# Masked softmax of x·W: another start order, strided transposes, and 16 KB runs over four batches

## The chip, the cores and the metric

The kernel runs on one core of a Trainium2 chip. The metric is the device time of one execution in microseconds (us). Instructions run on five engines: PE (matrix multiply, with its weight loads shown apart as PEld), DVE (VectorE), ACT (ScalarE), POOL (GpSimd) and SP (SyncE, which only issues transfers here). Transfers run on sixteen DMA engines.

## The reference

```python
batch, m, k, n = 16, 512, 512, 512          # x: (16,512,512) f32, weight: (512,512) f32
"scale": np.float32(0.125)
"mask": (np.triu(np.ones((m, n))) == 0).astype(np.float32)   # 1 strictly below the diagonal

y = scale * np.matmul(x, weight)
y = np.where(mask == 1, y, -1e9)
y_max = np.max(y, axis=-1, keepdims=True)
y_exp = np.exp(y - y_max)
return (y_exp / np.sum(y_exp, axis=-1, keepdims=True)).astype(np.float32)
```

Row 0 of every batch is masked everywhere, so its softmax is 1/512 in every column. In rows 0 to 255 the columns from 256 on are masked and their result is zero.

## The kernel before

**Units.** The work is cut into 16 units of 512 rows. A unit takes one half `h` (256 rows) of two neighbouring batches. Partition `2p+e` of the unit's tile holds four consecutive rows (`T = 4`) of batch `e`, so that one partition reads and writes one run of 4 x 2 KB = 8 KB in DRAM. Even units are the upper half (`h = 0`), for which only the first 256 columns of the product are computed ("narrow"); odd units are the lower half, with all 512 ("wide").

**Steps of a unit.** `load` (L78) brings 1 MB of x as float32. `cast` (L83, DVE) makes it bfloat16. `transpose` (L92, PE) makes 16 transposes of 128x128: each loads a slice of `xb` as the stationary operand and streams the identity through. `evict` copies them from PSUM to `xt`, half on DVE (L102), half on ACT (L103). `multiply` makes, for each of the four row slots, four matmuls with W (L116), one with the identity as stationary operand that adds -512 where the mask is 0 (L125, from `band`), and the exponential on ACT with the row sum (L135); no maximum is subtracted. `normalise` (DVE, L150 and L152) multiplies by the reciprocal of the sum and, in narrow units, POOL writes 1/512 into row 0 (L154). `store` (L158) writes 1 MB, with zeros in the columns that narrow units don't compute, which were put there once.

**Order.** The order on each engine is the program's order (`seq`). The main loop makes, for each `u`: transpose(u+1), cast(u+2), evict(u+1), multiply(u), normalise(u-1), store(u-1), load(u+7). All transfers are issued by SP, so they stand in one order: x's unit 0, W, the mask's diagonal blocks, x's units 1 to 7, and then stores and loads by turns.

**Start.** POOL builds the identity, the matrix `spread` (eight selections, L173), fills `band` with its constants (L182, L183) and four output tiles with zeros (L185, L186). W is loaded with row `kt*128+p` in partition `p`, that is four runs of 2 KB a partition, and cast in four pieces, two on DVE (L193), two on ACT (L195). The four 128x128 blocks on the mask's diagonal come in one DMA; `diag_bf` (L197) turns 0/1 into -512/0, and four matmuls with `spread` (L209) bring its rows to the partitions where the row slots of a unit stand; DVE and ACT copy them to `band` (L216).

**Buffers.** Eight x tiles and eight output tiles of 1 MB, three each of `xb` and `xt`, four PSUM banks for the transposes and four for the products.

Of the kernel before, what the change touches and what calls it, by code (L numbers as in the profile page):

```python
# [8 lines left out]
FP32 = mybir.dt.float32  # L9
BF16 = mybir.dt.bfloat16  # L10
AF = mybir.ActivationFunctionType
ALU = mybir.AluOpType

MASK_NEG = -512.0
P = 128
X_BUFS = 8
OUT_BUFS = 8


@with_exitstack  # L20
def kernel(
    ctx: ExitStack,
    tc: tile.TileContext,
    x: bass.AP,
    weight: bass.AP,
    scale: float,
    mask: bass.AP,
    out: bass.AP,
):

    nc = tc.nc  # L40

    B, M, K = x.shape
    K2, N = weight.shape
    assert K == K2 and N == 512 and K == 512 and M == 512 and B % 2 == 0
    KT = K // P
    T = 4
    HP = P // 2
    HB = 2 * P
    U = B

    const = ctx.enter_context(tc.tile_pool(name="const", bufs=1))
    x_pool = ctx.enter_context(tc.tile_pool(name="xf", bufs=X_BUFS))
    xb_pool = ctx.enter_context(tc.tile_pool(name="xb", bufs=3))
    xt_pool = ctx.enter_context(tc.tile_pool(name="xt", bufs=3))
    sum_pool = ctx.enter_context(tc.tile_pool(name="sums", bufs=4))
    psum_t = ctx.enter_context(tc.tile_pool(name="psum_t", bufs=4, space=bass.MemoryType.PSUM))
    psum_y = ctx.enter_context(tc.tile_pool(name="psum_y", bufs=4, space=bass.MemoryType.PSUM))

    x_r = x.rearrange("(c e) (h p t) k -> c h p e (t k)", e=2, h=2, t=T)
    out_r = out.rearrange("(c e) (h p t) n -> c h p e (t n)", e=2, h=2, t=T)  # L60

    diag_r = bass.AP(tensor=mask.tensor, offset=mask.offset, ap=[[N, P], [P * N + P, KT], [1, P]])

    ident_bf = const.tile([P, P], BF16, name="ident_bf")
    w_f32 = const.tile([P, KT, N], FP32, name="w_f32")
    w_bf = const.tile([P, KT, N], BF16, name="w_bf")
    diag_f32 = const.tile([P, KT, P], FP32, name="diag_f32")
    diag_bf = const.tile([P, KT, P], BF16, name="diag_bf")
    spread = const.tile([P, T, P], BF16, name="spread")
    band = const.tile([P, 2, T, HB], BF16, name="band")  # L70
    ots = [const.tile([P, T, N], FP32, name=f"ot{i}") for i in range(OUT_BUFS)]

    st_x, st_xb, st_pt, st_xt, st_sum = {}, {}, {}, {}, {}
    seq = tc.keep_in_program_order

    def load(u):
        xf = x_pool.tile([P, T, K], FP32, name="xf")
        seq(nc.sync.dma_start(xf.rearrange("p t k -> p (t k)"), x_r[u // 2, u % 2]))  # L78
        st_x[u] = xf

    def cast(u):
        xb = xb_pool.tile([P, T, K], BF16, name="xb")
        seq(nc.vector.tensor_copy(xb, st_x.pop(u)))  # L83
        st_xb[u] = xb

    def transpose(u):
        xb = st_xb.pop(u)
        st_pt[u] = [psum_t.tile([P, 2, T, P], BF16, name="pt") for _ in range(2)]
        for kt in range(KT):
            for t in range(T):  # L90
                seq(
                    nc.tensor.transpose(  # L92
                        st_pt[u][kt // 2][:, kt % 2, t],
                        xb[:, t, kt * P : (kt + 1) * P],
                        ident_bf,
                    )
                )

    def evict(u):
        xt = xt_pool.tile([P, KT, T, P], BF16, name="xt")  # L100
        pt = st_pt.pop(u)
        seq(nc.vector.tensor_copy(xt[:, 0:2], pt[0]))  # L102
        seq(nc.scalar.copy(xt[:, 2:4], pt[1]))  # L103
        st_xt[u] = xt

    def multiply(u):
        h = u % 2
        NC = (h + 1) * HB
        xt = st_xt.pop(u)
        ot = ots[u % OUT_BUFS]  # L110
        rsum = sum_pool.tile([P, T], FP32, name="rsum")
        for t in range(T):
            py = psum_y.tile([P, N], FP32, name="py")
            for kt in range(KT):
                seq(
                    nc.tensor.matmul(  # L116
                        py[:, :NC],
                        lhsT=xt[:, kt, t],
                        rhs=w_bf[:, kt, :NC],
                        start=(kt == 0),  # L120
                        stop=(kt == KT - 1),
                    )
                )
            seq(
                nc.tensor.matmul(  # L125
                    py[:, h * HB : NC],
                    lhsT=ident_bf,
                    rhs=band[:, h, t],
                    start=False,
                    stop=True,  # L130
                    skip_group_check=True,
                )
            )
            seq(
                nc.scalar.activation(  # L135
                    out=ot[:, t, :NC],
                    in_=py[:, :NC],
                    func=AF.Exp,
                    bias=0.0,
                    scale=float(scale),  # L140
                    accum_out=rsum[:, t : t + 1],
                )
            )
        st_sum[u] = rsum

    def normalise(u):
        ot = ots[u % OUT_BUFS]
        NC = (u % 2 + 1) * HB
        rinv = sum_pool.tile([P, T], FP32, name="rinv")
        seq(nc.vector.reciprocal(rinv, st_sum.pop(u)))  # L150
        for t in range(T):
            seq(nc.vector.tensor_scalar_mul(ot[:, t, :NC], ot[:, t, :NC], rinv[:, t : t + 1]))  # L152
        if u % 2 == 0:
            seq(nc.gpsimd.memset(ot[0:2, 0, :HB], 1.0 / N))  # L154

    def store(u):
        ot = ots[u % OUT_BUFS]
        seq(nc.sync.dma_start(out_r[u // 2, u % 2], ot.rearrange("p t n -> p (t n)")))  # L158


    load(0)
    seq(nc.sync.dma_start(w_f32, weight.rearrange("(kt p) n -> p kt n", p=P)))
    seq(nc.sync.dma_start(diag_f32, diag_r))
    for u in range(1, X_BUFS):
        load(u)

    make_identity(nc, ident_bf)


    nc.gpsimd.memset(spread, 0.0)  # L170
    for t in range(T):
        for g in range(2):
            nc.gpsimd.affine_select(  # L173
                out=spread[:, t, g * HP : (g + 1) * HP].rearrange("k (p e) -> k p e", e=2),
                in_=spread[:, t, g * HP : (g + 1) * HP].rearrange("k (p e) -> k p e", e=2),
                pattern=[[-4, HP // 2], [0, 2]],
                base=-t,
                channel_multiplier=1,
                compare_op=ALU.not_equal,
                fill=1.0,  # L180
            )
    nc.gpsimd.memset(band[:HP, :, :, P:], MASK_NEG)  # L182
    nc.gpsimd.memset(band[HP:, :, :, :P], 0.0)  # L183
    for i in range(0, OUT_BUFS, 2):
        nc.gpsimd.memset(ots[i][:, :, HB:], 0.0)  # L185
        nc.gpsimd.memset(ots[i][0:2, 0, HB:], 1.0 / N)  # L186

    cast(0)
    transpose(0)
    evict(0)  # L190
    for kt in range(KT):
        if kt % 2 == 0:
            seq(nc.vector.tensor_copy(w_bf[:, kt], w_f32[:, kt]))  # L193
        else:
            seq(nc.scalar.copy(w_bf[:, kt], w_f32[:, kt]))  # L195
    seq(
        nc.vector.tensor_scalar(  # L197
            out=diag_bf,
            in0=diag_f32,
            scalar1=-MASK_NEG,  # L200
            scalar2=MASK_NEG,
            op0=ALU.mult,
            op1=ALU.add,
        )
    )
    for t in range(T):
        pm = psum_y.tile([P, N], FP32, name="py")
        seq(
            nc.tensor.matmul(  # L209
                pm, lhsT=spread[:, t], rhs=diag_bf.rearrange("k b c -> k (b c)"), start=True, stop=True  # L210
            )
        )
        for g, copy in enumerate((nc.vector.tensor_copy, nc.scalar.copy)):
            half = slice(g * HP, (g + 1) * HP)
            src = pm.rearrange("p (h g c) -> p h g c", h=2, g=2)
            seq(copy(band[half, :, t, g * P : (g + 1) * P], src[half, :, g]))  # L216
    cast(1)

    for u in range(U + 1):
        if u + 1 < U:  # L220
            transpose(u + 1)
        if u + 2 < U:
            cast(u + 2)
        if u + 1 < U:
            evict(u + 1)
        if u < U:
            multiply(u)
        if u >= 1:
            normalise(u - 1)
            store(u - 1)  # L230
            if u - 1 + X_BUFS < U:
                load(u - 1 + X_BUFS)


# [33 lines left out]
```

The softmax here doesn't subtract the row's maximum and nothing guards it: scores larger than these inputs give would overflow.

## Time and profile before

| | |
|---|---|
| median of 12 runs | 93.08 us (91.92 to 94.42) |
| the profiled execution's own time | 94.23 us |
| its span, first to last instruction | 91.9 us |
| busy: PE, DVE, ACT, POOL | 68.2, 59.9, 54.4, 15.9 us |
| moved by DMA | 34.95 MB, mean 380 GB/s |
| HBM read, written | 18.09 MB, 16.78 MB |

The profiled execution took 2.33 us more than its span. The page gives busy time for each engine, then the span in 40 slices with a digit for each (9 is 90% or more), then the DMA queues, and the chain of work that ended last. A window row gives, for one stretch of the span, the busy time of PE, PEld, DVE, ACT and POOL (with the number of instructions), the granted PE clock, the mean busy share of the DMA engines and what they moved in GB/s. A row of the chain gives start, duration, and what ran. The time to landing of a DMA runs from its issue to the completion of its last byte.

### The profile page before, as it was taken

To read this page: it belongs to the slowest core of one execution; us is meant where nothing else is said; L and a number is where in the kernel's file an instruction comes from. 1 tells how busy PE (TensorE), PEld (TensorE's weight loads), DVE (VectorE), ACT (ScalarE), POOL (GpSimd) and SP (SyncE) were. 2 spreads that over 40 slices of the span, in tenths; PEclk is the share of its full clock that TensorE was granted. 3 is DMA by queue.
4 is the path that set the end of the run, shared out by engine and by line. 5 is a ranking of instruction groups with operands and counts; after the bars stand their busy time and mean duration, and the time that the engine had idled before them with its cause. 6 is when DMAs were issued, how large, how long until landed. Compare 5 with 4: busy or idle time off the path is not lost.

```text
span 91.9 us, 1608 instructions
## 1 busy us (share of the span) xinstructions
PE 68.2 (74%) x580; PEld 48.4 (53%) x580; DVE 59.9 (65%) x119; ACT 54.4 (59%) x151; POOL 15.9 (17%) x33
## 2 busy tenths in 40 slices
PE   0005216699999999999999999999999999930000
PEld 0005201678569758956964984795597587510000
DVE  0045979950939995995998699599394987525000
ACT  5000716066778777887877778697687779650000
POOL 7999960000100010010001001001000010100000
PEclk9999999999999999999999999999999999999855
DMA  1889999999999999999999999999999999999920
GB/s 29 321 294 339 383 424 431 421 435 417 424 417 367 396 417 364 349 414 424 403 449 403 449 403 435 414 439 414 439 417 428 417 435 417 428 428 385 417 114 11
DMA packets 5670, 34.95 MB, mean 380 GB/s; under 512 B 544, under 2 KB 1056, under 8 KB 1568
## 3 DMA queue, kind: packets, MB, share of 16 engines
q1 hardware_dynamic: 5664, 34.87, 93.2%
q8 instruction: 4, 0.07, 0.3%
q14 instruction: 2, 0.02, 0.0%
HBM read 18.09 MB, written 16.78 MB: 379 GB/s over the span
## 4 chain that ended last, share of the span: by engine, by line
PE 72%; DVE 11%; DMA 6%; ACT 1%; DVEq 0%; issue 0%; ACTq 0%
PE py L116 47%; PE pt L92 17%; PE py L125 8%; DMA xf<-in_x_dram 6%; DVE xb L83 3%; DVE w_bf L193 3%; DVE band L216 2%; DVE ot L152 1%; DVE xt L102 1%; PE py L209 1%; ACT ot L135 1%; DVE diag_bf L197 1%; DVEq L263 0%; DVE rinv L150 0%; ACTq L263 0%
## 5 line engine op out<-in xcount | busy, mean ns | idle before, releaser
L116 PE MATMUL py<-w_bf,xt 128*128 128x256 bf16 (+1 forms) x256 | 50.9, 333 | 0.0
L135 ACT ACTIVATE ot<-py 128x256 f32<-128x256 f32 (+1 forms) x64 | 31.2, 492 | 8.7 <-PE py L125 8.4
L116 PEld LDWEIGHTS <-xt 128*128 128x128 bf16 x256 | 25.1, 101 | 12.5
L83 DVE CAST xb<-xf 128x2048 bf16<-128x2048 f32 x16 | 20.2, 1264 | 8.8 <-DMA xf<-in_x_dram 8.8
L92 PE MATMUL pt<-ident_bf,xb 128*128 128x128 bf16 x256 | 18.6, 231 | 9.6 <-DVE xb L83 9.6
L103 ACT COPY xt<-pt 128x1024 bf16<-128x1024 bf16 x16 | 16.2, 1012 | 15.5 <-PE pt L92 11.2
L152 DVE TENSOR_SCALAR ot<-ot,rinv 128x256 f32<-128x256 f32 (+1 forms) x64 | 23.5, 430 | 0.8
L92 PEld LDWEIGHTS <-xb 128*128 128x128 bf16 x256 | 16.9, 104 | 11.5 <-DVE xb L83 10.5
L102 DVE COPY xt<-pt 128x1024 bf16<-128x1024 bf16 x16 | 11.0, 688 | 10.6 <-PE pt L92 10.6
L125 PE MATMUL py<-band,ident_bf 128*128 128x256 bf16 x64 | 17.8, 278 | 0.0
L154 POOL MEMSET ot<- 2x256 f32 x8 | 3.6, 449 | 62.5 <-DVE ot L152 62.5
L135 ACT ACTIVATION_READ_ACCUMULATOR ot<-py 128x1 f32 x64 | 12.8, 200 | 0.0
L125 PEld LDWEIGHTS <-ident_bf 128*128 128x128 bf16 x64 | 6.4, 100 | 4.3
L150 DVE RECIPROCAL rinv<-rsum 128x4 f32<-128x4 f32 x16 | 2.7, 169 | 3.2 <-ACT ot L135 3.2
L185 POOL MEMSET ot<- 128x1024 f32 x4 | 4.6, 1186 | 0.1
L209 PE MATMUL py<-diag_bf,spread 128*128 128x512 bf16 x4 | 1.9, 622 | 3.5 <-DVE diag_bf L197 3.5
L173 POOL TENSOR_SCALAR_AFFINE_SELECT spread<-spread 128x64 bf16<-128x64 bf16 x8 | 3.2, 440 | 0.0
L193 DVE CAST w_bf<-w_f 128x512 bf16<-128x512 f32 x2 | 3.1, 1612 | 0.0
L216 ACT CAST band<-py 64x256 bf16<-64x256 f32 x4 | 1.5, 367 | 2.7 <-DVE band L216 2.5
L209 PEld LDWEIGHTS <-spread 128*128 128x128 bf16 x4 | 0.6, 140 | 4.2 <-POOL ot L186 3.7
L216 DVE CAST band<-py 64x256 bf16<-64x256 f32 x4 | 1.7, 417 | 0.7 <-PE py L209 0.7
L103 ACT ACT_TABLE_LOAD x1 | 1.3, 1283 | 0.7 <-PEq L249 0.7
(12 smaller groups left out, 6.8 us busy)
## 6 DMA issues: line engine op xcount, KB each, us to landing
xf<-in_x_dram SPq DMA_DIRECT2D x16, 1024.0 KB, 14.2
out_dram<-ot SPq DMA_DIRECT2D x16, 1024.0 KB, 11.1
w_f<-in_weight_dram SPq DMA_DIRECT2D x1, 1024.0 KB, 8.0
diag_f<-in_mask_dram SPq DMA_DIRECT2D x1, 256.0 KB, 8.4
```

The lines of the kernel that those rows point to most:

```text
L83: seq(nc.vector.tensor_copy(xb, st_x.pop(u)))
L92: nc.tensor.transpose(st_pt[u][kt // 2][:, kt % 2, t], xb[:, t, kt * P : (kt + 1) * P], ident_bf,)
L102: seq(nc.vector.tensor_copy(xt[:, 0:2], pt[0]))
L103: seq(nc.scalar.copy(xt[:, 2:4], pt[1]))
L116: nc.tensor.matmul(py[:, :NC], lhsT=xt[:, kt, t], rhs=w_bf[:, kt, :NC], start=(kt == 0), stop=(kt == KT - 1),)
L125: nc.tensor.matmul(py[:, h * HB : NC], lhsT=ident_bf, rhs=band[:, h, t], start=False, stop=True, skip_group_check=True,)
L135: nc.scalar.activation(out=ot[:, t, :NC], in_=py[:, :NC], func=AF.Exp, bias=0.0, scale=float(scale), accum_out=rsum[:, t : t + 1],)
L152: seq(nc.vector.tensor_scalar_mul(ot[:, t, :NC], ot[:, t, :NC], rinv[:, t : t + 1]))
L154: seq(nc.gpsimd.memset(ot[0:2, 0, :HB], 1.0 / N))
L185: nc.gpsimd.memset(ots[i][:, :, HB:], 0.0)
L193: seq(nc.vector.tensor_copy(w_bf[:, kt], w_f32[:, kt]))
L216: seq(copy(band[half, :, t, g * P : (g + 1) * P], src[half, :, g]))
```

## The change

It has two groups of edits.

*The start.* The mask's diagonal blocks are loaded by four DMAs ahead of W, each block to 16 partitions with eight rows to a partition (`diag_f32` is now 64 partitions x 8 rows). `spread` now has 64 partitions and is made by four copies of a part of the identity on ACT. The zeros of the output tiles are written by DVE, while POOL keeps `band` and the rows of 1/512. PE makes twelve matmuls on a tile of zeros before its first transpose (`spin`). W is loaded with rows `4p` to `4p+3` in partition `p`, one run of 8 KB, and cast by one copy each on DVE and ACT after `band` is made. To fit this order of W's rows, the transposes take every fourth column of `xb` (`"p (k kt) -> p kt k"`) instead of 128 neighbouring ones.

*The runs.* A group now takes one half of four neighbouring batches, with eight consecutive rows (`S = 8`) in a partition: one run of 16 KB, 2 MB in all. It is computed as two units of four slots as before, so two narrow units are followed by two wide ones. There are five x tiles and four output tiles of 2 MB, and two instead of three of `xb` and `xt`. The first group is loaded in two halves, the second behind W. The first and the last group are stored in two halves, the others in one DMA after their second unit.

```diff
--- before.py
+++ after.py
@@ -13,8 +13,8 @@
 MASK_NEG = -512.0
 P = 128
-X_BUFS = 8
-OUT_BUFS = 8
+X_BUFS = 5
+OUT_BUFS = 4
 @with_exitstack
@@ -37,50 +37,56 @@
     nc = tc.nc
     B, M, K = x.shape
     K2, N = weight.shape
-    assert K == K2 and N == 512 and K == 512 and M == 512 and B % 2 == 0
+    assert K == K2 and N == 512 and K == 512 and M == 512 and B % 4 == 0
     KT = K // P
+    E = 4
+    S = 8
     T = 4
     HP = P // 2
     HB = 2 * P
-    U = B
+    G = B // 2
+    U = 2 * G
     const = ctx.enter_context(tc.tile_pool(name="const", bufs=1))
     x_pool = ctx.enter_context(tc.tile_pool(name="xf", bufs=X_BUFS))
-    xb_pool = ctx.enter_context(tc.tile_pool(name="xb", bufs=3))
-    xt_pool = ctx.enter_context(tc.tile_pool(name="xt", bufs=3))
+    xb_pool = ctx.enter_context(tc.tile_pool(name="xb", bufs=2))
+    xt_pool = ctx.enter_context(tc.tile_pool(name="xt", bufs=2))
     sum_pool = ctx.enter_context(tc.tile_pool(name="sums", bufs=4))
     psum_t = ctx.enter_context(tc.tile_pool(name="psum_t", bufs=4, space=bass.MemoryType.PSUM))
     psum_y = ctx.enter_context(tc.tile_pool(name="psum_y", bufs=4, space=bass.MemoryType.PSUM))
-    x_r = x.rearrange("(c e) (h p t) k -> c h p e (t k)", e=2, h=2, t=T)
-    out_r = out.rearrange("(c e) (h p t) n -> c h p e (t n)", e=2, h=2, t=T)
-    diag_r = bass.AP(tensor=mask.tensor, offset=mask.offset, ap=[[N, P], [P * N + P, KT], [1, P]])
+    x_r = x.rearrange("(c e) (h p t) k -> c h p e (t k)", e=E, h=2, t=S)
+    out_r = out.rearrange("(c e) (h p t) n -> c h p e (t n)", e=E, h=2, t=S)
     ident_bf = const.tile([P, P], BF16, name="ident_bf")
     w_f32 = const.tile([P, KT, N], FP32, name="w_f32")
     w_bf = const.tile([P, KT, N], BF16, name="w_bf")
-    diag_f32 = const.tile([P, KT, P], FP32, name="diag_f32")
-    diag_bf = const.tile([P, KT, P], BF16, name="diag_bf")
-    spread = const.tile([P, T, P], BF16, name="spread")
-    band = const.tile([P, 2, T, HB], BF16, name="band")
-    ots = [const.tile([P, T, N], FP32, name=f"ot{i}") for i in range(OUT_BUFS)]
+    diag_f32 = const.tile([HP, S, P], FP32, name="diag_f32")
+    diag_bf = const.tile([HP, S, P], BF16, name="diag_bf")
+    spread = const.tile([HP, 2, P], BF16, name="spread")
+    zeros = const.tile([P, N], BF16, name="zeros")
+    band = const.tile([P, 2, S, HB], BF16, name="band")
+    ots = [const.tile([P, S, N], FP32, name=f"ot{i}") for i in range(OUT_BUFS)]
     st_x, st_xb, st_pt, st_xt, st_sum = {}, {}, {}, {}, {}
     seq = tc.keep_in_program_order
-    def load(u):
-        xf = x_pool.tile([P, T, K], FP32, name="xf")
-        seq(nc.sync.dma_start(xf.rearrange("p t k -> p (t k)"), x_r[u // 2, u % 2]))
-        st_x[u] = xf
+    def slots(u):
+        return slice(T * (u % 2), T * (u % 2) + T)
+    def load(g, part=slice(0, S)):
+        if g not in st_x:
+            st_x[g] = x_pool.tile([P, S, K], FP32, name="xf")
+        run = slice(part.start * K, part.stop * K)
+        seq(nc.sync.dma_start(st_x[g].rearrange("p t k -> p (t k)")[:, run], x_r[g // 2, g % 2][:, :, run]))
     def cast(u):
         xb = xb_pool.tile([P, T, K], BF16, name="xb")
-        seq(nc.vector.tensor_copy(xb, st_x.pop(u)))
+        seq(nc.vector.tensor_copy(xb, st_x[u // 2][:, slots(u)]))
         st_xb[u] = xb
     def transpose(u):
@@ -91,7 +97,7 @@
                 seq(
                     nc.tensor.transpose(
                         st_pt[u][kt // 2][:, kt % 2, t],
-                        xb[:, t, kt * P : (kt + 1) * P],
+                        xb[:, t].rearrange("p (k kt) -> p kt k", kt=KT)[:, kt],
                         ident_bf,
                     )
                 )
@@ -104,10 +110,10 @@
         st_xt[u] = xt
     def multiply(u):
-        h = u % 2
+        h = u // 2 % 2
         NC = (h + 1) * HB
         xt = st_xt.pop(u)
-        ot = ots[u % OUT_BUFS]
+        ot = ots[u // 2 % OUT_BUFS][:, slots(u)]
         rsum = sum_pool.tile([P, T], FP32, name="rsum")
         for t in range(T):
             py = psum_y.tile([P, N], FP32, name="py")
@@ -125,7 +131,7 @@
                 nc.tensor.matmul(
                     py[:, h * HB : NC],
                     lhsT=ident_bf,
-                    rhs=band[:, h, t],
+                    rhs=band[:, h, slots(u)][:, t],
                     start=False,
                     stop=True,
                     skip_group_check=True,
@@ -144,55 +150,61 @@
         st_sum[u] = rsum
     def normalise(u):
-        ot = ots[u % OUT_BUFS]
-        NC = (u % 2 + 1) * HB
+        ot = ots[u // 2 % OUT_BUFS][:, slots(u)]
+        NC = (u // 2 % 2 + 1) * HB
         rinv = sum_pool.tile([P, T], FP32, name="rinv")
         seq(nc.vector.reciprocal(rinv, st_sum.pop(u)))
         for t in range(T):
             seq(nc.vector.tensor_scalar_mul(ot[:, t, :NC], ot[:, t, :NC], rinv[:, t : t + 1]))
-        if u % 2 == 0:
-            seq(nc.gpsimd.memset(ot[0:2, 0, :HB], 1.0 / N))
-    def store(u):
-        ot = ots[u % OUT_BUFS]
-        seq(nc.sync.dma_start(out_r[u // 2, u % 2], ot.rearrange("p t n -> p (t n)")))
-    load(0)
-    seq(nc.sync.dma_start(w_f32, weight.rearrange("(kt p) n -> p kt n", p=P)))
-    seq(nc.sync.dma_start(diag_f32, diag_r))
-    for u in range(1, X_BUFS):
-        load(u)
+        if u % 4 == 0:
+            seq(nc.gpsimd.memset(ot[0:E, 0, :HB], 1.0 / N))
+    def store(g, part=slice(0, S)):
+        ot = ots[g % OUT_BUFS]
+        run = slice(part.start * N, part.stop * N)
+        seq(nc.sync.dma_start(out_r[g // 2, g % 2][:, :, run], ot.rearrange("p t n -> p (t n)")[:, run]))
+    load(0, slots(0))
+    DP = P // S
+    for b in range(KT):
+        r = b * P
+        seq(
+            nc.sync.dma_start(
+                diag_f32[b * DP : (b + 1) * DP],
+                mask[r : r + P, r : r + P].rearrange("(p t) c -> p t c", t=S),
+            )
+        )
+    seq(nc.sync.dma_start(w_f32, weight.rearrange("(p kt) n -> p kt n", kt=KT)))
+    load(0, slots(1))
+    for g in range(1, X_BUFS):
+        load(g)
+    nc.vector.memset(zeros, 0.0)
+    def spin(n):
+        idle = psum_y.tile([P, N], FP32, name="py")
+        for _ in range(n):
+            seq(nc.tensor.matmul(idle, lhsT=zeros[:, :P], rhs=zeros, start=True, stop=True))
+    spin(12)
     make_identity(nc, ident_bf)
-    nc.gpsimd.memset(spread, 0.0)
-    for t in range(T):
-        for g in range(2):
-            nc.gpsimd.affine_select(
-                out=spread[:, t, g * HP : (g + 1) * HP].rearrange("k (p e) -> k p e", e=2),
-                in_=spread[:, t, g * HP : (g + 1) * HP].rearrange("k (p e) -> k p e", e=2),
-                pattern=[[-4, HP // 2], [0, 2]],
-                base=-t,
-                channel_multiplier=1,
-                compare_op=ALU.not_equal,
-                fill=1.0,
-            )
     nc.gpsimd.memset(band[:HP, :, :, P:], MASK_NEG)
     nc.gpsimd.memset(band[HP:, :, :, :P], 0.0)
     for i in range(0, OUT_BUFS, 2):
-        nc.gpsimd.memset(ots[i][:, :, HB:], 0.0)
-        nc.gpsimd.memset(ots[i][0:2, 0, HB:], 1.0 / N)
+        nc.vector.memset(ots[i][:, :, HB:], 0.0)
+        nc.gpsimd.memset(ots[i][0:E, 0, HB:], 1.0 / N)
+    for e in range(E):
+        seq(nc.scalar.copy(spread.rearrange("k h (q e) -> k (h q) e", e=E)[:, :, e], ident_bf[:HP, :HP]))
     cast(0)
     transpose(0)
     evict(0)
-    for kt in range(KT):
-        if kt % 2 == 0:
-            seq(nc.vector.tensor_copy(w_bf[:, kt], w_f32[:, kt]))
-        else:
-            seq(nc.scalar.copy(w_bf[:, kt], w_f32[:, kt]))
     seq(
         nc.vector.tensor_scalar(
             out=diag_bf,
@@ -203,17 +215,28 @@
             op1=ALU.add,
         )
     )
-    for t in range(T):
-        pm = psum_y.tile([P, N], FP32, name="py")
-        seq(
-            nc.tensor.matmul(
-                pm, lhsT=spread[:, t], rhs=diag_bf.rearrange("k b c -> k (b c)"), start=True, stop=True
-            )
-        )
-        for g, copy in enumerate((nc.vector.tensor_copy, nc.scalar.copy)):
-            half = slice(g * HP, (g + 1) * HP)
-            src = pm.rearrange("p (h g c) -> p h g c", h=2, g=2)
-            seq(copy(band[half, :, t, g * P : (g + 1) * P], src[half, :, g]))
+    for h in range(2):
+        for j in range(2):
+            pm = psum_y.tile([P, N], FP32, name="py")
+            seq(
+                nc.tensor.matmul(
+                    pm,
+                    lhsT=spread[:, h],
+                    rhs=diag_bf[:, slots(j)].rearrange("k t c -> k (t c)"),
+                    start=True,
+                    stop=True,
+                )
+            )
+            for g, copy in enumerate((nc.vector.tensor_copy, nc.scalar.copy)):
+                half = slice(g * HP, (g + 1) * HP)
+                seq(
+                    copy(
+                        band[half, h, slots(j), g * P : (g + 1) * P],
+                        pm.rearrange("p (t c) -> p t c", t=T)[half],
+                    )
+                )
+    seq(nc.vector.tensor_copy(w_bf[:, 0:2], w_f32[:, 0:2]))
+    seq(nc.scalar.copy(w_bf[:, 2:4], w_f32[:, 2:4]))
     cast(1)
     for u in range(U + 1):
@@ -227,9 +250,13 @@
             multiply(u)
         if u >= 1:
             normalise(u - 1)
-            store(u - 1)
-            if u - 1 + X_BUFS < U:
-                load(u - 1 + X_BUFS)
+            g, second = divmod(u - 1, 2)
+            if g in (0, G - 1):
+                store(g, slots(u - 1))
+            elif second:
+                store(g)
+            if second and g + X_BUFS < G:
+                load(g + X_BUFS)
 # ---- launch: one core; inputs and outputs as the reference has them ----
```

## The prediction, made before the result was known

> **What bounds the kernel now.** I read the page's busy shares and slices first, then the DMA queue, the chain, and the start and the tail in windows of half a microsecond. From the page:
>
> ```profile
> PE 68.2 (74%) x580; PEld 48.4 (53%) x580; DVE 59.9 (65%) x119; ACT 54.4 (59%) x151; POOL 15.9 (17%) x33
> ...
> DMA  1889999999999999999999999999999999999920
> ...
> q1 hardware_dynamic: 5664, 34.87, 93.2%
> ...
> PE 72%; DVE 11%; DMA 6%; ACT 1%; DVEq 0%; issue 0%; ACTq 0%
> ```
>
> The chain names PE (72%), and PE is busy without a gap from 16.86 to 81.3 us. But the DMA engines are full from 3 to 88 us, and 34.87 MB at the plateau of 426 GB/s is 81.9 us. Two limits run side by side. Which ends last is read from SP's waits, the landing of the stores, and the tail (last columns: DMA share, GB/s):
>
> ```profile
> SPq L263 <- DMA out_dram<-ot: 6.3, 1, 6.3
> ```
> ```profile
> DMA to landing us min/median/max: 6.6/11.1/16.8
> ```
> ```profile
> 84.00:84.50 0.50, 0.00 (x0) 0.00 (x0) 0.00 (x0) 0.00 (x0) 0.00 (x0) 1.00 1.01 426
> 84.50:85.00 0.50, 0.00 (x0) 0.00 (x0) 0.00 (x0) 0.00 (x0) 0.00 (x0) 1.00 0.58 246
> 85.00:85.50 0.50, 0.00 (x0) 0.00 (x0) 0.00 (x0) 0.00 (x0) 0.00 (x0) 1.00 0.86 360
> ...
> 88.00:88.50 0.50, 0.00 (x0) 0.00 (x0) 0.00 (x0) 0.00 (x0) 0.00 (x0) 0.50 0.24 98
> 89.00:89.50 0.50, 0.00 (x0) 0.00 (x0) 0.00 (x0) 0.00 (x0) 0.00 (x0) 0.50 0.08 33
> ```
>
> A 1 MB store needs 2.46 us at 426 GB/s, yet its median landing is 11.1 us: it stands in a queue. The last one is issued at 84.0 us, just as that queue runs dry (246 GB/s at 84.5), flows until about 87.8, and one engine (33 GB/s is about one sixteenth) trails to 90.5. So the kernel is balanced: a faster PE alone wins only the dry moment, a PE slower by a microsecond shows. The start, in DMA windows and in the chain:
>
> ```profile
> 5.00:5.50 0.50, 0.00 (x0) 0.00 (x0) 0.00 (x0) 0.00 (x0) 0.50 (x1) 1.00 0.85 283
> 5.50:6.00 0.50, 0.00 (x0) 0.00 (x0) 0.08 (x1) 0.00 (x0) 0.45 (x2) 1.00 0.67 172
> 8.50:9.00 0.50, 0.50 (x8) 0.50 (x6) 0.00 (x0) 0.00 (x0) 0.50 (x2) 1.00 0.93 270
> 9.00:9.50 0.50, 0.50 (x7) 0.50 (x6) 0.49 (x1) 0.00 (x0) 0.50 (x1) 1.00 0.62 148
> ```
> ```profile
> 0.74 5.15 DMA xf<-in_x_dram
> 5.92 1.98 DVE xb L83
> ...
> 9.71 3.06 DVE w_bf L193 x2
> 12.77 0.54 DVE diag_bf L197
> ...
> 16.86 1.89 PE pt L92 x16
> ...
> 22.41 0.89 PE pt L92 x16
> ```
>
> The first two windows are the change from x to W (2 KB pieces), the other two the mask (512 B pieces). In the chain, sixteen transposes cost 1.89 us at 16.86 and 0.89 at 22.41: PE starts slow and doubles.
>
> [...]
>
> **The change part by part**, against the profiled execution: 94.23 us, 2.33 of it outside its span of 91.9. The median of the runs shown is 93.08, so I apply the difference to that.
>
> *Supply of DMA.* Bytes stay. By 9.7 us before has moved x's first MB, W and mask (2.36 MB; the windows summed from 0). In the change the first MB of x is unchanged (over at 5.4 us). The mask becomes four DMAs of 16 partitions, each with four more issues of about 0.6 us on SP ahead of W; these hide under x's 2.4 us. Its 0.26 MB would take 1.25 us at the 209 GB/s of the windows 8.5 to 9.5[...]. I take 1.5[...]. W in 8 KB pieces: 1.05 MB / 426 GB/s = 2.46 us. Sum 5.4 + 1.5 + 2.46 = 9.36, against 9.7: -0.3 us[...].
>
> *16 KB runs.* W's 2 KB pieces ran at 414, 369, 414 and 348 GB/s from 6.5 to 8.5 us, mean 386, or 84.9 ns a piece on one of 16 engines; 8 KB at 426 is 307.7 ns. The two give about 10.6 ns fixed a piece, and 1.7% for doubling 8 KB[...]. 27.3 MB are in 16 KB runs (33.6 less the first group's load and store and the last group's store in halves): [...]-0.7 us (between 0 and -1.1).
>
> *The dry moment at the tail*: (426-246)/426 x 0.5 + (426-360)/426 x 0.5 = 0.3 us, gone if the last store is issued before the queue is empty. Is it? The chain's start shrinks. cast(0) took 1.98 us beside POOL's fills, the other casts 1.22; POOL now has two band fills of twice the size (2 x 0.95 each), some 3.8 us, done near 5.2, and DVE two output fills, under 5 us at POOL's 1.19 us for 1024 elements, hidden by x's landing at 5.9. T(0) ends near 8.1; DVE then evicts (0.69), makes diag (0.65, mask landed about 7.6), four band copies of 512 (0.69 by the eviction's slope) and half of W (0.65): about 13.1, ACT's half of W at 14.1. x's second MB, now behind W, lands about 12.5, cast(1) ends at 14.3. T(1) thus starts 2.5 us before 16.86. But slots 2 and 3 come in one 2 MB load that lands near 17.5, cast(2) ends at 18.7, and T(2), 22.25 before, can't start earlier. Twelve zero matmuls keep PE warm to about 6; between 8 and 14 us PE has only four matmuls, and I expect it to be cold again at T(1): 1.89, then a cold M(0) of 4.2, so T(2) starts near 20.5. PE then ends about 79.5 and the last store is issued near 82.3. DMA by then still holds about 4 us of work (its end, 87.8 less the terms of this sum, is 86.5). So -0.3 us, and neither warming nor the shorter start is worth more.
>
> *At nothing.* Two xb and xt buffers instead of three: the wait added to cast(u+2) is for T(u), one unit earlier on PE; behind that cast stand evict(u+1) and normalise(u-1), neither wanted before T(u+1). Narrow units now come in twos: PE 3.08 us each against DVE 3.6 (1.22+0.69+0.17+4x0.38), a lag of 1 us a pair, inside the following M and T (3.1 us) and worked off in the wide pair (4.78 against 4.0). Stores of 2 MB wait for two units: up to 4.8 us later, under a backlog of the same size; if that cover goes, the DMA queue dries once per group. *Strided transposes*: weight loads read every fourth bf16, 8 bytes apart[...]. Cost from 0 (the load is beside the matmul: 0.89/16 = 56 ns a pair)[...]. I take 0.
>
> Sum: -0.3 - 0.7 - 0.3 = -1.3 us; 93.08 - 1.3 = 91.8.
>
> **Rivals.**
> 1. *The DMA wins more*: the slack in the mixed stage (windows of 287 at 29 us, 270 to 385 from 34 to 38) also shrinks with fewer changes between reads and writes. About 1.3 us is lost there; with -1.1 for runs and -0.6 at the start: 90.0. Against: later mixed windows already run at 420.
> 2. *Nothing is left*: [...]runs give -0.3, tail -0.3: 93.2.
> 3. *Slower: strided weight loads.* Place: the 16 transposes of each unit.[...] It decides once the last store is issued after 84.0, 1.7 us of slack / (14 x 16) = 8 ns a transpose; for 1% slower about 12 ns. For: loads and matmuls alternate at 56 ns with little room. Against: [...]PEld is busy 53% only.
> 4. *Slower DMA*: 16 KB pieces unbalance the sixteen queues by half a piece-time a DMA; +1 us, 94.1.
>
> **How the numbers follow.** Forecast 0.52 (its own range 90.9 to 92.8), rival 1 0.20, rival 2 0.10, rival 3 0.12, rival 4 0.06. About 1% is what a measurement here can tell from no change. The range 89.6 to 95.0 holds all but the strided case and the far end of rival 1. Faster by over 1%: 0.41 of the forecast and 0.19 of rival 1; within 1%: the rest of these and rival 2; slower: rivals 3 and 4.
>
> **What would show it.** Right: plateau near 430 GB/s, W landed by 10 us, transposes still 0.89 us for sixteen, last store issued with GB/s full until the end. Wrong: sixteen transposes over 1 us (rival 3)[...], gaps in the DMA row in mid-run (the cover of the 2 MB stores is gone).

## The result, and the profile after

The changed kernel takes 90.99 us (median of 11 runs, 90.74 to 91.41). Its ratio to the kernel before is 0.9866, with a 95% interval of 0.9838 to 0.9895: 1.25 us faster, where 1.3 us were forecast. One thing must be known to read the numbers: executions of the kernel before spread from 91.6 to 94.8 us (those of the changed kernel from 90.7 to 91.4), the profile shown of it (94.23) is one of the long ones, and the ratios leave those out (what the ratio above counts averages 92.2), so that the medians (93.22 and 90.99) differ by more than the ratio says.

The page of the changed kernel, with the lines that answer to those shown of before:

```profile
PE 71.2 (80%) x592; PEld 48.8 (55%) x592; DVE 60.7 (68%) x121; ACT 55.9 (63%) x154; POOL 6.6 (7%) x14
...
DMA  0999999999999999999999999999999999999940
...
q1 hardware_dynamic: 3456, 34.87, 94.3%
q8 instruction: 4, 0.07, 0.3%
...
PE 73%; DVE 9%; DMA 6%; issue 1%; ACT 1%; DVEq 1%; ACTq 0%
```

The bytes are as before, in 3456 packets for 5664, and the share of the DMA queue is 94.3% for 93.2%. POOL has lost the selections and the fills of the output tiles. The chain names PE with 73% again (72% before); the experiments show that it is not PE that sets the end. Start and tail in windows of half a microsecond (last columns: DMA share, GB/s):

```profile
5.50:6.00 0.50, 0.50 (x3) 0.09 (x1) 0.00 (x0) 0.00 (x0) 0.28 (x1) 1.00 1.04 239
7.00:7.50 0.50, 0.00 (x0) 0.00 (x0) 0.50 (x1) 0.00 (x0) 0.00 (x0) 1.00 0.76 246
...
85.00:85.50 0.50, 0.00 (x0) 0.00 (x0) 0.00 (x0) 0.00 (x0) 0.00 (x0) 0.50 0.85 360
86.50:87.00 0.50, 0.00 (x0) 0.00 (x0) 0.00 (x0) 0.00 (x0) 0.00 (x0) 0.50 0.20 82
87.00:87.50 0.50, 0.00 (x0) 0.00 (x0) 0.00 (x0) 0.00 (x0) 0.00 (x0) 0.50 0.16 66
```

The mask and the first part of W flow at 239 to 249 GB/s from 5.5 to 7.5 us. At the end there is the trail again: 82 and 66 GB/s are about three of sixteen engines, by an estimate from the plateau (426 / 16 = 26.6 GB/s each). The chain shows the transposes of three units:

```profile
14.34 1.90 PE pt L98 x16
...
19.04 1.04 PE pt L98 x16
...
22.26 0.89 PE pt L98 x16
```

Sixteen strided transposes cost 0.89 us on a warm PE (at 22.26 us), as the contiguous ones did (0.89 at 22.41 before). T(1) starts at 14.34 instead of 16.86 and is cold, 1.90 us for its sixteen; T(2) starts at 18.99 instead of 22.25, as the timeline has it. The last store is issued at 80.8 instead of 84.0 us.

The bytes moved, summed over such windows, divide the span. 2.36 MB are x's first MB, W and mask; the whole is 34.9 MB. The last column is each execution's own time less its span, the median over all runs of the kernel.

| kernel (us) | 2.36 MB at | 2.36 to 33 MB | 33 to 34.8 MB | 34.8 MB to end of span | span | outside the span |
|---|---|---|---|---|---|---|
| before | 9.65 | 73.5 | 4.6 | 4.2 | 91.9 | 2.34 |
| before, ten x tiles | 9.79 | 72.2 | 4.8 | 2.6 | 89.3 | 2.31 |
| before, no mask matmuls | 10.05 | 72.1 | 4.6 | 2.9 | 89.7 | 2.34 |
| changed | 9.28 | 72.2 | 4.5 | 3.3 | 89.2 | 1.80 |
| changed, second profile | 9.52 | 71.7 | 4.8 | 3.3 | 89.3 | 1.77 |
| start edits alone | 9.14 | 72.4 | 4.5 | 3.0 | 89.0 | 1.81 |
| runs alone | 9.71 | 72.3 | 5.5 | 2.0 | 89.5 | 2.02 |
| transfers alone, 8 KB | 9.79 | 71.8 | 4.3 | 1.8 | 87.6 | 1.79 |
| transfers alone, 16 KB and the changed order | 9.32 | 71.4 | 4.4 | 2.3 | 87.4 | 1.79 |

### The profile page after: what moved, and what is told of

Its sections match the earlier page's. It is cut to its first block, busy times and chain, and to the rows that moved or that the text cites. A ratio compares the mean times of both kernels' runs of the same rounds, so it can differ in the third digit from the quotient of the medians.

```text
span 89.2 us, 1590 instructions
## 1 busy us (share of the span) xinstructions
PE 71.2 (80%) x592; PEld 48.8 (55%) x592; DVE 60.7 (68%) x121; ACT 55.9 (63%) x154; POOL 6.6 (7%) x14
## 3 DMA queue, kind: packets, MB, share of 16 engines
q1 hardware_dynamic: 3456, 34.87, 94.3%
## 4 chain that ended last, share of the span: by engine, by line
PE 73%; DVE 9%; DMA 6%; issue 1%; ACT 1%; DVEq 1%; ACTq 0%
PE py L122 47%; PE pt L98 17%; PE py L131 8%; DMA xf<-in_x_dram 6%; DVE band L233 3%; DVE xb L89 3%; DVE ot L158 1%; DVE diag_bf L209 1%; DVE w_bf L238 1%; ACT ot L141 1%; DVEq L290 0%; PE py L222 0%; DVE rinv L156 0%; ACTq L290 0%; DVEq L209 0%
## 5 line engine op out<-in xcount | busy, mean ns | idle before, releaser
L122 PE MATMUL py<-w_bf,xt 128*128 128x256 bf16 (+1 forms) x256 | 50.0, 329 | 0.0
L98 PE MATMUL pt<-ident_bf,xb 128*128 128x128 bf16 x256 | 17.8, 225 | 4.8 <-DVE xb L89 4.8
L160 POOL MEMSET ot<- 4x256 f32 x4 | 1.8, 448 | 62.9 <-DVE ot L158 62.9
L190 PE MATMUL py<-zeros 128*128 128x512 bf16 x12 | 5.3, 632 | 1.2 <-DVE zeros L185 1.2
L198 DVE MEMSET ot<- 128x2048 f32 x2 | 3.5, 1765 | 0.8 <-issue 0.8
L190 PEld LDWEIGHTS <-zeros 128*128 128x128 bf16 x12 | 1.6, 144 | 3.9 <-issue 2.8
L233 ACT CAST band<-py 64x512 bf16<-64x512 f32 x4 | 2.3, 580 | 1.1 <-DVE band L233 1.0
L233 DVE CAST band<-py 64x512 bf16<-64x512 f32 x4 | 2.5, 675 | 0.5 <-PE py L222 0.5
L196 POOL MEMSET band<- 64x2048 bf16 x1 | 1.8, 1799 | 0.1
L195 POOL MEMSET band<- 64x2048 bf16 x1 | 1.8, 1802 | 0.0
L222 PE MATMUL py<-diag_bf,spread 64*128 64x512 bf16 x4 | 1.0, 374 | 0.9 <-DVE diag_bf L209 0.9
```

The costliest lines, as they stand in the source:

```text
L98: nc.tensor.transpose(st_pt[u][kt // 2][:, kt % 2, t], xb[:, t].rearrange("p (k kt) -> p kt k", kt=KT)[:, kt], ident_bf,)
L122: nc.tensor.matmul(py[:, :NC], lhsT=xt[:, kt, t], rhs=w_bf[:, kt, :NC], start=(kt == 0), stop=(kt == KT - 1),)
L190: seq(nc.tensor.matmul(idle, lhsT=zeros[:, :P], rhs=zeros, start=True, stop=True))
L198: nc.vector.memset(ots[i][:, :, HB:], 0.0)
L233: copy(band[half, h, slots(j), g * P : (g + 1) * P], pm.rearrange("p (t c) -> p t c", t=T)[half],)
```

## The experiments

### Each half of the change alone

The start edits on the kernel before, whose units and 8 KB runs stay (the mask's blocks then take 32 partitions each, with four rows):

```diff
 load(0)
-W: weight.rearrange("(kt p) n -> p kt n", p=P), then the mask in one DMA
+mask in four DMAs, then W: weight.rearrange("(p kt) n -> p kt n", kt=KT)
+zeros, spin(12); fills of the output tiles on DVE; spread by copies of the identity
-xb[:, t, kt * P : (kt + 1) * P]
+xb[:, t].rearrange("p (k kt) -> p kt k", kt=KT)[:, kt]
```

> The kernel before with only the start edits of the change (mask in four DMAs ahead of W, W in 8 KB pieces with strided transposes, fills on DVE, zero matmuls); units, 8 KB runs and buffers stay. Theory (DMA queue sets the end; start gives 0.3 us of supply and the tail's dry moment 0.3 us): 0.6 us under the kernel before, ratio about 0.993. Rival (the start, by letting PE begin earlier, is what made it faster): the whole 1.2 us, ratio 0.987. Rival (16 KB runs are all of it): ratio 1.000.

Measured: 90.63 us (6 runs, 90.55 to 90.85), ratio 0.9806 (0.9742 to 0.9871). The start alone brings all that the change brings, and the forecast share of 0.6 us for it was too small.

The changed kernel with its start undone:

```diff
-mask in four DMAs, W in 8 KB pieces, spin(12), fills on DVE, strided transposes
+W second, in 2 KB pieces; the mask in one DMA behind it; spread by 16 selections on POOL
+fills on POOL; contiguous transposes; eight matmuls with spread instead of four
```

> The change with its start undone (W second and in 2 KB pieces, the mask in one DMA behind it, selections and fills on POOL, contiguous transposes, no zero matmuls); the 16 KB runs, the groups of 2 MB and the buffers stay. Theory: the runs' 0.7 us, and with PE starting as late as before or later no tail gain: ratio about 0.993. Rival (16 KB runs are all of it): 0.987. Rival (the start is all of it): 1.000 or a little slower, since eight row slots need sixteen selections.

Measured: 91.87 us (22 runs, 91.26 to 94.32), ratio 0.9922 (0.9886 to 0.9957). By itself this half looks as forecast. But 0.3 of its 0.7 us lies outside the span (2.02 against 2.34), which no transfer inside the span explains, and the halves don't add up: 0.9806 x 0.9922 would be 0.973. So the next question was what 16 KB runs are worth as transfers.

### The transfers alone

All computation is left out; the loads and stores stand in the order of the kernel that each run is made from:

```diff
-    cast, transpose, evict, band, multiply, normalise
+    for i in range(OUT_BUFS):
+        nc.vector.memset(ots[i], 0.0)
     for u in range(U):
         store(u)
         if u + X_BUFS < U:
             load(u + X_BUFS)
```

> The transfers of the kernel before alone: the same loads and stores in the same order with 8 KB runs, no computation at all, stores take constant tiles. Theory (the queue is full from 3 us on and sets the end): 34.87 MB at 426 GB/s is 81.9 us plus about 3 us before and 2 behind, a span of 87 and a time of 89 to 90 us, only 2 to 3 us under the kernel before. Rival (PE sets the end and the queue only looks full): 86 us or less.

> The transfers of the changed kernel alone, in 16 KB runs (the first and last groups' halves as well as in the others stay as in it but the stores are whole groups); no computation. Theory[...]: 0.7 us under the same with 8 KB runs. Rival (no fixed part, runs cost the same): within 0.2 us of it. Rival (10.6 ns a piece): 1.1 us or more under it.

Measured: 89.39 us with 8 KB (89.21 to 89.42) and 89.57 with 16 KB (89.13 to 90.96); the ratio to the kernel before is 0.967 for both. The first is the floor that was expected of a full queue: the changed kernel is 1.6 us above it. The second run has not only the longer pieces but also the changed order of the mask and W, since it is made from the changed kernel. So both together bring the bare transfers nothing; apart they were not run. The fixed part of a piece is there: in the packet records of the two traces a piece of 8 KB takes 309 ns and one of 16 KB 611 ns (medians), 7 ns less than twice as much. The table shows where it goes: with 16 KB, 2.36 MB are moved 0.5 us earlier and the middle is 0.4 us shorter, but from 34.8 MB to the end of the span it takes 2.3 us against 1.8: with 16 KB the flow fades from 328 over 131 to 33 GB/s in three windows of half a microsecond, with 8 KB from 344 to 33 in two. The stretch from 33 to 34.8 MB is 0.1 us longer, and the span of the two profiles differs by 0.2 us.

### Is it PE or the queue?

```diff
-            seq(nc.tensor.matmul(py[:, h * HB : NC], lhsT=ident_bf, rhs=band[...], ...))   # L125 / L131
```

> The changed kernel without the same 64 matmuls (the mask is left out of the result), PE 7 us shorter. Theory (the DMA queue alone sets the end now): within 0.3 us of the changed kernel's 91.0. Rival (PE still sets it): 2 us or more under 91.0.

> The kernel before without the 64 matmuls that add the mask (L125), so the mask is left out of the result; PE has 64 x 0.11 = 7 us less to do, its start is unchanged. Theory (two limits: the queue sets the pace, and the late start of PE leaves its last stores uncovered): the tail is covered, the thin stretch at 28 to 38 us stays, 0.5 to 1 us under the kernel before. Rival (PE's pace sets the end): 4 us or more under it. Rival (only the thin stretch counts): no change.

Measured: the changed kernel without these matmuls takes 90.76 us (90.28 to 91.12): 5 us of busy time taken from the engine that the chain names (71.2 to 66.2; the estimate was 7) give 0.2 us. PE doesn't even end much earlier: its last matmul ends at 77.5 us for 78.1, while the casts that it needs now wait longer for x. The kernel before without these matmuls has a median of 92.61 and runs from 91.62 to 94.03. Its ratio of 0.9795 (0.9704 to 0.9886) compares with a chip on which the kernel before took 92.89 at the least; on other chips that kernel took as little as 91.6, and nothing of 4 us shows. In neither kernel does PE's pace set the end.

Page line of the changed kernel without them, and the waits of the casts in the changed kernel and in this one (us, times, longest):

```profile
PE 66.2 (74%) x528; PEld 43.7 (49%) x528; DVE 60.6 (68%) x121; ACT 55.2 (62%) x154; POOL 6.7 (7%) x14
```
```profile
DVE xb L89 <- DMA xf<-in_x_dram: 7.2, 4, 3.4
```
```profile
DVE xb L89 <- DMA xf<-in_x_dram: 11.4, 5, 3.5
```

### The slow stretch from 28 to 38 us

```diff
-X_BUFS = 8
+X_BUFS = 10
```

> The kernel before with ten x tiles instead of eight, nothing else: 2 MB more of loads stand in the queue before the first store. Theory (before, the first stores are issued at 25 us, just as the eight loads have drained, and the queue runs thin from 28 to 38 us, which the windows of 287 and 270 GB/s show): the thin stretch goes, about 1.5 us under the kernel before where that stretch was thin, ratio 0.985 to 0.993. Rival (that stretch is the price of mixing reads and writes): ratio 1.000.

Windows of 2 us, first the kernel before, then this one:

```profile
28.00:30.00 2.00, 2.00 (x22) 1.79 (x19) 1.97 (x6) 1.82 (x6) 0.00 (x0) 1.00 0.98 332
34.00:36.00 2.00, 2.00 (x24) 1.50 (x23) 0.88 (x2) 1.38 (x4) 0.00 (x0) 1.00 1.01 365
36.00:38.00 2.00, 2.00 (x21) 1.79 (x19) 1.97 (x7) 1.97 (x7) 0.00 (x0) 1.00 1.02 328
```
```profile
28.00:30.00 2.00, 2.00 (x26) 1.85 (x25) 2.00 (x5) 2.00 (x9) 0.00 (x0) 1.00 0.98 410
34.00:36.00 2.00, 2.00 (x28) 1.88 (x27) 1.20 (x4) 1.47 (x4) 0.00 (x0) 1.00 1.04 438
36.00:38.00 2.00, 2.00 (x28) 1.87 (x26) 2.00 (x5) 1.85 (x9) 0.00 (x0) 1.00 0.99 418
```

The stretch is gone, and 91.77 us is measured, 91.63 to 91.95 in six runs. Its ratio of 0.9779 (0.9717 to 0.9841) says too much, since the shortest run of the kernel before was 92.89 on that chip and 91.6 on others: against the shortest of those, this edit gains nothing. The stretch isn't the price of mixing loads and stores, because this kernel mixes them too. But the theory of a queue run thin isn't shown either. The DMA share stays at 0.98 to 1.02 in the slow windows: the packets took longer, the engines weren't idle. And the kernel without mask matmuls, whose first store is issued at 24.37 us into a queue of eight loads, has a profile without the stretch. What decides on it stays open. How much of the 1.25 us it makes up is not shown: the executions of the kernel before that the ratio counts average 92.2 us and begin at 91.6. Inside the span the kernel with ten x tiles, whose start is that of before, takes 89.3 to 89.7 us in its six runs, and the changed kernel 89.0 to 89.6; apart from the stretch, then, little of the gain seems to lie inside the span.

### The trail at the end

The transfers alone with 8 KB, and 576 matmuls that nothing waits for:

```diff
+    for u in range(U):
+        idle = psum_y.tile([P, N], FP32, name="py")
+        for _ in range(36):
+            seq(nc.tensor.matmul(idle[:, :P], lhsT=diag_bf[:, 0], rhs=w_bf[:, 0, :P], start=True, stop=True))
```

> The transfers of the kernel before alone, as in the run of that kind with 8 KB runs, with 576 matmuls on constant tiles beside them that nothing waits for: about as many PE instructions as in the real kernels. All real kernels show a queue of instruction packets (0.07 MB), and one DMA engine that trails by 2 to 3 us at the end; the bare transfers show neither. Theory (the packets sit on one DMA engine, whose share of the data is thus late by 0.07 MB / 26.6 GB/s = 2.6 us): the instruction queue and the trail appear, 1.5 to 2.5 us over the 89.4 of the bare transfers. Rival (the trail comes from waits for computed stores): no trail, 89.4.

Measured: 90.58 us (90.53 to 90.79) for 89.39. A queue appears that the bare transfers don't have, and the end changes. From the page, and two windows of each, without and with the matmuls:

```profile
q8 instruction: 4, 0.07, 0.3%
```
```profile
86.00:86.50 0.50, 0.00 (x0) 0.00 (x0) 1.00 0.09 33
86.50:87.00 0.50, 0.00 (x0) 0.00 (x0) 1.00 0.00 0
```
```profile
86.00:86.50 0.50, 0.00 (x0) 0.00 (x0) 0.00 (x0) 0.00 (x0) 0.50 0.27 115
86.50:87.00 0.50, 0.00 (x0) 0.00 (x0) 0.00 (x0) 0.00 (x0) 0.50 0.31 131
```

So the 1.2 us come with PE's instructions, not with waits for computed stores. Whether fetching the instructions costs them or running them is not shown. It is less than the 1.5 to 2.5 us expected, and 131 GB/s is more than one engine's 26.6 (the same estimate as above): that the packets sit on a single engine is not shown either. The start edits alone (90.63) stand at this floor.

### The two best side by side, the issue of W, and the zero matmuls

> The changed kernel as it is, run beside the others of this call: 90.7 to 91.4 us, as in its first runs.

> The start edits with 8 KB runs, once more and on the chip of the changed kernel. Theory (16 KB runs bring nothing once the start feeds the queue): 90.4 to 90.9 us, 0.2 to 0.4 us under the changed kernel. Rival (the first comparison was one between chips): the same as the changed kernel within 0.1 us.

Measured on one chip: the changed kernel 90.92 us (90.75 to 91.10), the start edits with 8 KB runs 90.54 (90.46 to 90.58). The ranges don't meet: the second group of edits costs some 0.4 us on top of the first. In the two profiles the difference arises ahead of 2.36 MB (8.87 us for the start edits, 9.52 changed). The mask's blocks also differ there, 16 partitions against 32; no run tells that apart from the longer pieces.

```diff
-    seq(nc.sync.dma_start(w_f32, ...))      # behind the mask
+    seq(nc.scalar.dma_start(w_f32, ...))    # ACT's first instruction, in start_alone
```

> The start edits with 8 KB runs, and W's load issued by ACT as its first instruction instead of by SP behind the mask. Theory (the supply between 2 and 9 us has holes, 66 GB/s at 2.5 us in the kernel before and about 250 behind x's first MB, that a second issuing queue can fill; the queue sets the end): 2.36 MB moved by 8.6 instead of 9.1 us and 0.3 to 0.6 us under the start edits alone. Rival (x's first MB now shares the engines with W, lands 2 us later and PE starts later): 0 to 1 us slower.

Measured: 90.9 us (90.51 to 92.99), no gain. W now flows beside x's first MB, at 410 to 475 GB/s from 5 to 7 us where the start edits alone have 252 to 312, and then the mask has the engines for itself:

```profile
8.00:8.50 0.50, 0.00 (x0) 0.00 (x0) 0.21 (x1) 0.00 (x0) 0.00 (x0) 0.63 0.55 105
8.50:9.00 0.50, 0.00 (x0) 0.00 (x0) 0.50 (x1) 0.00 (x0) 0.00 (x0) 0.50 0.51 112
```

2.36 MB are moved at 9.28, no earlier than before the edit: what W won, the uncovered mask lost.

```diff
-    spin(12)
```

> The changed kernel without its twelve zero matmuls. Theory (PE is cold again at T(1) in any case, and the queue sets the end): T(0)'s transposes take about 1.9 instead of 1.0 us, the time stays within 0.2 us. Rival (a warm start counts): 0.5 us or more slower.

Measured: 90.62 us (90.28 to 91.18), 0.3 us below the changed kernel's 90.92, whose range (90.75 to 91.10) lies within this one. T(0)'s sixteen transposes take 1.90 us for 1.08 (from the start of the first to the end of the last in the timeline), and T(1) is cold in both (1.90): the zero matmuls warm one unit's transposes and no time is won by it.

## Why the prediction was right

The forecast of 91.8 against 93.08, -1.3 us, met -1.25 us. What bounds the kernel was read rightly, but that the sum met the number is luck: of its three terms one failed, one doesn't show, one shows in its place but not in the time, and 0.54 us of the gain was in none of them. As a time, 91.8 lay 0.8 us above the 90.99 measured.

*The bound.* That the DMA queue and not the chain's PE sets the end holds: the transfers alone take 89.39 us, and 5 us less of busy PE give 0.2 us.

*Supply, -0.3 us.* Right in its place: with the start of before, 2.36 MB are moved at 9.65 to 10.05 us in four profiles with compute; with the mask and W in the new order at 8.87 to 9.53 in six. That the end comes earlier by it is not shown: the bare transfers move 2.36 MB at 9.32 for 9.79 us with the new order and take no less time. The mask's slow stage was priced at 1.5 us, the author's estimate, above the 1.25 us that the windows of before give. In the changed kernel it overlaps with W, and the two flow at 239 to 249 GB/s; where it stood alone, over 32 partitions, it flowed at 105 to 112. Blocks of 16 partitions were not run alone, so the 1.5 us is not shown. Rival 2's 93.2 counts a dearer mask, an estimate that no run shows either.

*16 KB runs, -0.7 us.* Wrong, and this is the term that failed. The 0.7 us was the author's estimate, below the 1.1 us that 10.6 ns a piece, from the windows of before, would make; the packet records show 7 ns. And the rate in the middle was taken for the end. The middle gains 0.4 us in bare transfers, which the longer fading of the flow (2.3 us for 1.8) takes back, and on top of the start edits the second group costs 0.4 us. Rival 4's sense, that larger pieces unbalance the queues, fits this better, though no run tries it by itself. What the runs alone won, 0.7 us, is 0.3 outside the span, and the rest is no more than the kernel before varies by.

*Dry moment, -0.3 us.* The stretch from 33 to 34.8 MB is 4.6 us before and 4.5 and 4.8 in the two profiles after: nothing to see. The reading of 246 GB/s at 84.5 us as a queue run dry was weak, since the changed kernel shows 262 at 80.5 with 2 MB still to move:

```profile
80.50:81.00 0.50, 0.00 (x0) 0.00 (x0) 0.23 (x1) 0.00 (x0) 0.00 (x0) 1.00 0.62 262
```

*What was missing.* 0.54 us of the gain lies outside the span: execution time less span is 2.31 to 2.34 us for the kernel before and its two variants with the same start, 1.77 to 1.84 for all with the new start and for the bare transfers, 2.02 for the runs alone. The forecast carried the 2.33 us of the profiled execution over unchanged. The start edits alone bring all of it. The order of the loads is not what does it, since the bare transfers in the order of before are at 1.79, nor are the zero matmuls, since the changed kernel without them is at 1.80. Which of the others it is, and whether it lies ahead of the first instruction or behind the last, was not tried and stays open.

*The schedule.* The forecast steps of PE held: cast(2) ending at 18.7 (18.9), T(1) at 14.35 and cold (14.34, 1.90 us), the end of PE at 79.5 (78.1), the last store at 82.3 (80.8). M(0) was expected cold throughout and turned warm at about 17.3 us (its first row slot took 1.06 us, the third 0.55), which gave 1.5 us that nobody needed.

*Strided transposes at 0.* Right: 0.89 us for sixteen. The weight loads did get longer, 113 ns for 98 (medians, changed kernel and before), but the pace of the pairs, 0.89 us / 16 = 56 ns in both, doesn't show it:

```profile
L92 PEld LDWEIGHTS <-xb x256: 97/98/152, 7.9 to 75.0; 128*128 128x128 bf16 x128
```
```profile
L98 PEld LDWEIGHTS <-xb x256: 112/113/147, 7.6 to 70.0; 128*128 128x128 bf16 x128
```

So weight loads that read every fourth bf16 keep the pace of the transposes here, 0.89 us for sixteen where rival 3 needed over 1 us. Rival 3 falls.

## What to carry to other kernels

Where the DMA share is full from end to end, run the transfers alone before pricing anything, and once more with as many matmuls beside them as the kernel has: their time is the floor (89.4 and 90.6 us here), and an edit that only moves compute, or one that lets PE start earlier, has the distance to it to win: here 5 us less of busy PE won 0.2 us of 1.6. Compare two such runs only if they differ in one thing; here one had both the longer pieces and another order of loads. Test each half of a combined change by itself, because halves that each look like a gain need not add up; here the kernel with the first half alone, at 90.54 us, beats the whole. And compare the execution's time less its span as well as the span: half a microsecond of this gain was there, and none of the forecast's terms looked for it.

## What was not expected of the hardware

- Doubling the run of a piece from 8 to 16 KB, with another order of the first loads, gave no faster transfers: 89.39 and 89.57 us for 34.87 MB, though a 16 KB piece took 7 ns less than two of 8 KB (611 against 309 ns each).
- 576 matmuls without any wait cost bare transfers 1.2 us, together with 0.07 MB of instruction packets; most of it shows at the end of the full queue, where 115 and 131 GB/s still flow from 86 to 87 us and 33 and 0 do without them.
- The mask's 512-byte rows, alone on the engines and in four transfers of 32 partitions each, flowed at 105 to 112 GB/s.
- Weight loads that read every fourth bf16 took 113 ns for 98, and sixteen transposes still 0.89 us.
